# A decoder trunk in float32: attention scores one step further ahead of their transposes, with a larger scratch ring for the weights

## The chip, the core and the metric

One core of one Trainium2 chip runs the whole program. The metric is device time in microseconds (us) of one execution, here the median of three runs. TensorE is called PE, its weight loads PEld, VectorE DVE, ScalarE ACT, GpSimd POOL, and SyncE (which only issues DMAs) SP.

## What is computed

Two layers, each of three blocks with a layer norm behind each: a SwiGLU feed-forward, a token mixer, a second SwiGLU feed-forward. The stream has 512 tokens of 1024 channels in float32. The change lies in the mixer alone. Its attention part, cut to what matters:

```python
# B: 12 heads of 64 in three dilated groups; A: 8 heads in 2 groups, selected and windowed keys
scores = q @ k.T * scale                  # per query block of 128
e = exp(scores - max) * mask
p = e / sum(e)                            # the attention weights
o = p @ v
# A's two branches are scaled by sigmoid gates and added, with a third over compressed keys;
# the groups of B are merged by their softmax denominators
```

Beside it the mixer has the input projections, a gated spatial unit (SGU), sigmoid gates over 3 x 1024 columns, and the merge. Every float32 product is made from halves: a high part rounded to fp32r and a low part, the remainder, so that one product is three matmuls (`mm3`, lines 461 to 463).

## The kernel before, in words

**Two streams in one.** `mixer` (1441) weaves two Python generators while the program is written out: `dense` (1415: compressed keys, B's projections for heads j = 0..3, A's for two groups, SGU, gates, merge) and `attn` (1424: the attention steps). `weave` (1461) emits one piece of attention, then dense pieces worth 1.5 (B) or 1.6 (A) times its estimated matmul time. If attention isn't ready, a dense piece is emitted; if dense can't go on, attention goes alone, and when both wait, the flag `force` lets attention skip its safety margin (960). Each engine executes its instructions in the order in which they were written, so this order is what counts.

**An attention step** is one head and one query block i = 0..3 of 128 rows. `pipe` (962) runs 16 B steps (j, i), then 32 A steps (h, i). One turn n of `pipe` does, in this order:

- the transposes of an older step m (`turn`, 966), if no P·V is pending;
- the scores of step n: matmuls on PE, masking and row minimum on DVE into a float32 tile E (B line 1549, A line 1652), then exp on ACT (1566, 1667);
- `finish` (971): a pending P·V (`pv`), m's transposes if still open, and `low(m)`: DVE's subtraction that makes the low half of the transposed weights (1602, 1704). The transposes' high half is an ACT cast (1593, 1691). When m has i = 3, the head's P·V is pending for the next turn;
- the normalisation of E by POOL (`scale`; 1572 for B in the same turn, 1676 for A in the next one).

Which older step m is taken is set by `lag`: the step whose scores lie `lag` turns back. While the next step's projections aren't there and `force` is on, lines 990 to 993 finish all live steps one after the other, whatever `lag` says. This is called a drain below.

```python
m = live.popleft() if live and n - live[0]["turn"] >= live[0]["f"].lag else None
...
if self.force and (m or live or pv):
    yield from finish(m or (live.popleft() if live else None))
```

**Scratch.** `Fa` has 76 blocks of 128 columns, 44 of its own and 32 that hold the stream until it is spilled to DRAM. E tiles are taken in a ring from its start: blocks 0..`EB` in B, 0..`EA` in A (1525, 1640). Dense's temporaries (rope, SGU, gates, the P·V accumulator `ev`) use a ring over the rest, `f_lo` to 76 (329), where `f_lo` is `EB`, then `EA`. A B step takes 3, 6, 8 or 10 blocks for i = 0..3, an A step 2, 4, 6 or 8; they are freed when its transposes are written out (1595, 1693).

**Around it.** POOL also makes the low half of the streamed mixer weights (390), 1024 columns at a time, and adds in rope (918, 934, 1104, 1106).

Of the kernel before, what the change touches and what calls it, by code (L numbers as in the profile page):

```python
# [230 lines left out]

RB, R0, FB = 232, 152, 44
HB = RB - R0
EB, EA = 30, 24
XB = NT * KT
RAW, WB, LOOK = 3, 4, 8
MARGIN, RATIO_B, RATIO_A = 6.0, 1.5, 1.6
# [4 lines left out]
class Trunk:  # L242
# [719 lines left out]
    def pipe(self, steps):  # L962

        live, pv = deque(), None

        def turn(m):
            m["f"].transposes(m)
            m["turned"] = True
            yield m["f"].t_cost(m)

        def finish(m):
            nonlocal pv
            if pv:
                yield from pv["f"].pv(pv["step"])
                pv = None
            if m:
                if not m["turned"]:
                    yield from turn(m)
                m["f"].low(m)
                if m["step"][-1] == NT - 1:  # L980
                    pv = m

        for n, (f, step) in enumerate(steps + [(None, None)] * 4):
            if live and live[-1]["turn"] == n - 1 and live[-1]["f"].late:
                live[-1]["f"].scale(live[-1])
            m = live.popleft() if live and n - live[0]["turn"] >= live[0]["f"].lag else None
            if m and not pv:
                yield from turn(m)
            if f:
                while not f.ready(*step):  # L990
                    if self.force and (m or live or pv):
                        yield from finish(m or (live.popleft() if live else None))
                        m = None
                    else:
                        yield WAIT
                while (s := f.scores(*step)) is None:
                    yield WAIT
                s.update(f=f, step=step, turn=n, turned=False)
                live.append(s)
                self.ratio = f.ratio  # L1000
                yield f.s_cost(s)
                f.exps(s)
            yield from finish(m)
            if f and not f.late:
                f.scale(s)
        yield from finish(None)
# [499 lines left out]

class StepsB:

    lag, late, ratio = 2, 0, RATIO_B

    def __init__(self, t):
        self.t = t
# [112 lines left out]

class StepsA:

    lag, late, ratio = 3, 1, RATIO_A

    def __init__(self, t):  # L1630
        self.t = t
# [131 lines left out]
```

## Time and profile before

| | before |
|---|---|
| three runs | 2710.33, 2713.63, 2713.87 us |
| median | 2713.63 us |
| the profiled execution's own time | 2713.97 us |
| its span, first to last instruction | 2711.9 us |
| PE busy in the span | 96% |
| DVE, ACT, POOL busy | 65%, 45%, 45% |
| mean granted clock of PE | 0.989 of full speed |

The feed-forwards are dense matmul work and fill about 1.6 ms of the span. The two mixers lie at about 370 to 910 us and 1720 to 2280 us; the attention steps in them run from 428 to 800 us and from 1776 to 2150 us. A share of the span is an average over both kinds of stage, so the attention stretches are to be read by themselves.

### The profile page before, as it was taken

The page shows a single profiled execution, that of the slowest core. Times are in us where ns is not written, and L with a number is a line of the kernel's source. Part 1 is how long each engine was busy: PE and PEld are TensorE (multiplying, and loading weights), DVE is VectorE, ACT ScalarE, POOL GpSimd, SP SyncE. Part 2 cuts the span into 40 slices and gives each one's busy share as a digit, 9 for nine tenths or more (in the row PEclk, how much of TensorE's full clock was granted, in tenths as well). Part 3 has the DMA queues.
Part 4 walks back from the last instruction along what each step waited for, and adds up shares of the span by engine and source line. Part 5 has one row for each costly group of instructions (what it writes and reads, how often), then busy time and mean ns, then how long its engine had stood idle before and what let it go on. Part 6 is the DMA issues. An engine that isn't in the chain of part 4 may idle for free.

```text
span 2711.9 us, 42598 instructions
## 1 busy us (share of the span) xinstructions
PE 2611.7 (96%) x16302; PEld 2346.8 (87%) x16302; DVE 1776.2 (65%) x3155; ACT 1209.4 (45%) x2410; POOL 1223.9 (45%) x961
## 2 busy tenths in 40 slices
PE   8999999989999999999999999999899999999998
PEld 7999888877788888998889998888777888889987
DVE  6887565567552378885688875755674424698856
ACT  4555344345642235554345553334455422355542
POOL 4774025454645426770057720345446445277600
PEclk9999999999999999999999999999999999999999
DMA  3334322121212332333223342321112123323332
GB/s 132 102 110 144 100 98 96 37 71 39 71 42 85 108 132 86 109 102 126 77 86 110 102 134 91 110 77 60 47 40 74 45 91 115 118 94 102 109 117 78
DMA packets 71211, 248.68 MB, mean 92 GB/s; under 512 B 8016, under 2 KB 10096, under 8 KB 71008
## 3 DMA queue, kind: packets, MB, share of 16 engines
q1 hardware_dynamic: 68832, 238.25, 26.5%
q0 software_dynamic: 2176, 7.71, 0.9%
q8 instruction: 128, 2.10, 0.3%
q14 instruction: 75, 0.61, 0.1%
HBM read 239.64 MB, written 6.29 MB: 91 GB/s over the span
## 4 chain that ended last, share of the span: by engine, by line
PE 82%; DVE 11%; ACT 3%; issue 2%; POOL 2%; DMA 0%; DVEq 0%; ACTq 0%; SPq 0%; POOLq 0%
PE P L461 25%; PE P L462 25%; PE P L463 25%; DVE wl L390 2%; PE P L1722 1%; PE P L1615 1%; POOL wl L390 1%; DVE R L575 1%; DVE Fa L1549 1%; DVE Fa L631 1%; PE P L1686 1%; PE P L1651 1%; PE P L886 1%; ACT wh L387 1%; PE P L1588 1%
## 5 line engine op out<-in xcount | busy, mean ns | idle before, releaser
L461 PE MATMUL P<-R,wh 128*128 128x256 f32 (+1 forms) x2928 | 891.4, 304 | 8.0 <-ACT Fa L817 6.4
L463 PE MATMUL P<-R,wl 128*128 128x256 f32 (+1 forms) x2928 | 890.5, 304 | 6.9 <-DVE wl L390 6.4
L462 PE MATMUL P<-R,wh 128*128 128x256 f32 (+1 forms) x2928 | 888.6, 303 | 7.0 <-DVE R L541 6.9
L387 ACT CAST wh<-raw 128x1024 fp32r<-128x1024 f32 (+3 forms) x521 | 431.3, 833 | 508.4 <-PE P L463 248.1
L390 POOL TENSOR_TENSOR wl<-raw,wh 128x1024 fp32r<-128x1024 f32 (+4 forms) x159 | 357.2, 2254 | 660.8 <-ACT wh L387 660.2
L390 DVE TENSOR_TENSOR wl<-raw,wh 128x512 fp32r<-128x512 f32 (+2 forms) x363 | 422.2, 1166 | 312.5 <-ACT wh L387 312.2
L463 PEld LDWEIGHTS P<-R,wl 128*128 128x128 f32 x2928 | 560.9, 192 | 33.6 <-DVE wl L390 11.7
L461 PE MATMUL P<-wh,R 128*128 128x512 f32 (+3 forms) x1600 | 583.6, 365 | 6.5 <-DVE R L893 5.6
L461 PEld LDWEIGHTS P<-R,wh 128*128 128x128 f32 x2928 | 561.0, 192 | 32.8 <-ACT Fa L817 8.4
L462 PEld LDWEIGHTS P<-R,wh 128*128 128x128 f32 x2928 | 561.0, 192 | 30.2 <-DVE R L541 9.0
L463 PE MATMUL P<-wh,R 128*128 128x512 f32 (+3 forms) x1600 | 573.1, 358 | 4.4 <-DVE R L541 4.2
L462 PE MATMUL P<-wl,R 128*128 128x512 f32 (+3 forms) x1600 | 573.0, 358 | 4.1 <-POOL wl L390 2.1
L390 DVE TENSOR_TENSOR wl<-Fa,wh 128x512 fp32r<-128x512 f32 x304 | 353.1, 1163 | 87.0 <-ACT wh L387 87.0
L461 PEld LDWEIGHTS P<-wh,R 128*128 128x128 f32 x1600 | 305.0, 191 | 45.9 <-issue 6.6
L463 PEld LDWEIGHTS P<-wh,R 128*128 128x128 f32 x1600 | 304.2, 190 | 46.3 <-DVE R L541 5.3
L462 PEld LDWEIGHTS P<-wl,R 128*128 128x128 f32 x1600 | 304.9, 191 | 43.5 <-POOL wl L390 3.1
L408 POOL TENSOR_TENSOR Fa<-raw 128x512 f32<-128x512 f32 x152 | 227.0, 1493 | 194.5 <-DMA raw<-in_wts 96.5
L387 ACT CAST wh<-Fa 128x512 fp32r<-128x512 f32 x304 | 180.9, 617 | 4.4 <-POOL Fa L408 4.4
L834 ACT ACTIVATE Fa<-Fa 128x512 f32<-128x512 f32 x76 | 48.0, 632 | 242.3 <-DVE Fa L832 242.3
L408 POOL TENSOR_TENSOR Fa<-raw,Fa 128x512 f32<-128x512 f32 x76 | 131.9, 1735 | 3.7 <-DVE wl L390 3.7
L408 POOL TENSOR_TENSOR Fa<-Fa,raw 128x512 f32<-128x512 f32 x76 | 117.0, 1540 | 6.0
L1676 POOL TENSOR_SCALAR Fa<-Fa,ac,ga 128x128 f32<-128x128 f32 (+3 forms) x128 | 78.8, 627 | 84.4 <-DVE ac L1672 83.9
(222 smaller groups left out, 3144.4 us busy)
## 6 DMA issues: line engine op xcount, KB each, us to landing
raw<-in_wts SPq DMA_DIRECT2D x400, 512.0 KB, 3.3
raw<-in_wts SPq DMA_DIRECT2D x16, 480.0 KB, 3.2
x_sp<-Fa SPq DMA_DIRECT2D x8, 512.0 KB, 5.2
Fa<-x_sp SPq DMA_DIRECT2D x8, 512.0 KB, 5.3
Fa<-in_ln_g POOLq DMA_DIRECT2D x6, 512.0 KB, 4.4
Fa<-in_ln_b POOLq DMA_DIRECT2D x6, 512.0 KB, 5.6
raw<-in_wts SPq DMA_DIRECT2D x8, 320.0 KB, 3.0
Fa<-in_x SPq DMA_DIRECT2D x4, 512.0 KB, 7.2
```

The lines of the kernel that those rows point to most:

```text
L387: nc.scalar.copy(h, r)
L390: (nc.gpsimd if kind == "full" and (self.pool_lo or j == 1) else nc.vector).tensor_tensor(lo, r, hf, op=OP.subtract)
L408: self.nc.gpsimd.tensor_tensor(v, x, y, op=op)
L461: mm(out, lh, rh, start=start, stop=False, skip_group_check=more)
L462: mm(out, lh, rl, start=False, stop=False, skip_group_check=more)
L463: mm(out, ll, rh, start=False, stop=stop, skip_group_check=more)
L575: nc.vector.tensor_tensor(lo, t[n], hif, op=OP.subtract)
L631: self.nc.vector.scalar_tensor_tensor(xs[:, c], xs[:, c], r, b[:, c], op0=OP.mult, op1=OP.add)
L834: nc.scalar.activation(st["g"], st["g"], AF.Silu)
L886: self.nc.tensor.transpose(self.P[b][:s.shape[-1], k * 128:(k + 1) * 128], s, self.ident)
L1549: nc.vector.tensor_tensor_reduce(E[:, at:at + n], P, m, -SCALE, 3e38 if g == 0 else acc[:, g - 1:g], OP.add, OP.min, acc[:, g:g + 1])
L1676: t.nc.gpsimd.tensor_scalar(e, e, rd[:, br:br + 1], t.ga[:, s["i"], c:c + 1], op0=OP.mult, op1=OP.mult)
```

## The change

B's `lag` goes from 2 to 3 and A's from 3 to 4, so each step's transposes, casts, low halves and P·V are written one turn later against the scores. The E ring grows from 30 to 40 blocks in B and from 24 to 32 in A, and dense's ring, which starts where it ends, shrinks from 46 to 36 and from 52 to 44 blocks. `pipe` runs one empty turn more at its end. No instruction of the computation is added or taken away.

```diff
-EB, EA = 30, 24
+EB, EA = 40, 32
...
-        for n, (f, step) in enumerate(steps + [(None, None)] * 4):
+        for n, (f, step) in enumerate(steps + [(None, None)] * 5):
...
 class StepsB:
 
-    lag, late, ratio = 2, 0, RATIO_B
+    lag, late, ratio = 3, 0, RATIO_B
...
 class StepsA:
 
-    lag, late, ratio = 3, 1, RATIO_A
+    lag, late, ratio = 4, 1, RATIO_A
```

## Rows read from the trace of the kernel before

**Rows 1.** The page: busy us, share of the span, instructions; then the chain's shares.

```profile
PE 2611.7 (96%) x16302; PEld 2346.8 (87%) x16302; DVE 1776.2 (65%) x3155; ACT 1209.4 (45%) x2410; POOL 1223.9 (45%) x961
...
PE 82%; DVE 11%; ACT 3%; issue 2%; POOL 2%; DMA 0%; DVEq 0%; ACTq 0%; SPq 0%; POOLq 0%
```

**Rows 2.** PE's waits over the span: line, releaser: us in total, times, longest.

```profile
PE P L1615 <- DVE R L1602: 12.3, 4, 4.3
PE P L1588 <- POOL Fa L1572: 9.9, 8, 2.1
...
PE P L1722 <- DVE R L1704: 5.8, 10, 1.4
```

**Rows 3.** PE in time, B steps: start, us, instruction, [idle before, releaser], layer 1.

```profile
466.98 2.89 PE L1615 MATMUL P<-R,Rb 128*128 128x512 f32 x11 [1.92 <-DVE R L1602]
...
498.35 2.01 PE L1588 MATMUL P<-ident,Fa 128*128 128x128 f32 x10 [2.12 <-POOL Fa L1572]
...
518.98 0.67 PE L1588 MATMUL P<-ident,Fa 128*128 128x128 f32 x3 [1.99 <-DVE Rb L893]
...
533.96 1.31 PE L1588 MATMUL P<-ident,Fa 128*128 128x128 f32 x10 [1.09 <-POOL Fa L1572]
...
585.45 1.31 PE L1588 MATMUL P<-ident,Fa 128*128 128x128 f32 x10 [1.49 <-POOL Fa L1572]
...
598.65 6.17 PE L1615 MATMUL P<-R,Rb 128*128 128x512 f32 x23 [4.28 <-DVE R L1602]
```

**Rows 4.** Windows: start:end, us, busy PE, PEld, DVE, ACT, POOL, PE's clock, DMA.

```profile
460.00:472.00 12.00, 9.89 (x62) 8.32 (x60) 7.01 (x25) 4.94 (x11) 5.81 (x5) 0.86 0.25 82
496.00:502.00 6.00, 3.88 (x22) 3.66 (x20) 3.29 (x8) 1.97 (x5) 2.98 (x3) 0.73 0.39 139
532.00:538.00 6.00, 4.91 (x36) 4.60 (x36) 4.23 (x13) 2.97 (x9) 2.03 (x3) 1.00 0.01 3
```

**Rows 5.** POOL in time, around the second head's last B step.

```profile
491.80 2.28 POOL L390 TENSOR_TENSOR wl<-raw,wh 128x960 fp32r<-128x960 f32 x1
...
494.73 2.25 POOL L390 TENSOR_TENSOR wl<-raw,wh 128x960 fp32r<-128x960 f32 x1
496.95 1.34 POOL L1572 TENSOR_SCALAR Fa<-Fa,ac 128x1280 f32<-128x1280 f32 x1
```

**Rows 6.** PE in time: six transposes; one matmul of a projection.

```profile
439.21 0.90 PE L1588 MATMUL P<-ident,Fa 128*128 128x128 f32 x6
...
448.30 0.28 PE L461 MATMUL P<-wh,R 128*128 128x256 f32 x1
```

**Rows 7.** DVE in time, ahead of the fourth head's P·V.

```profile
592.90 2.14 DVE L1226 TENSOR_SCALAR ac<-ac 128x4 f32<-128x4 f32 x1
...
597.58 1.61 DVE L1602 TENSOR_TENSOR R<-P,R 128x256 fp32r<-128x256 f32 x3
```

**Rows 8.** POOL in time, the same stretch.

```profile
592.64 4.67 POOL L390 TENSOR_TENSOR wl<-raw,wh 128x1024 fp32r<-128x1024 f32 x2 [0.64 <-ACT wh L387]
```

**Rows 9.** PE in time, A steps: waits of transposes (1686) and of P·V (1722).

```profile
700.86 0.66 PE L1686 MATMUL P<-ident,Fa 128*128 128x128 f32 x4 [0.36 <-POOL Fa L1676]
...
701.85 0.66 PE L1686 MATMUL P<-ident,Fa 128*128 128x128 f32 x4 [0.33 <-POOL Fa L1676]
...
731.00 0.49 PE L1722 MATMUL P<-R 128*128 128x512 f32 x1 [0.73 <-ACT R L1691]
...
732.87 0.50 PE L1722 MATMUL P<-R 128*128 128x512 f32 x1 [1.38 <-DVE R L1704]
```

**Rows 10.** PE in time: the shortest and the longest scores of an A step.

```profile
583.40 0.56 PE L1651 MATMUL P<-R,Rb 128*128 128x128 f32 x4
...
631.20 1.17 PE L1651 MATMUL P<-R,Rb 128*128 128x512 f32 x4
```

**Rows 11.** DVE in time: one mask-and-minimum of an A step with 384 and with 512 columns.

```profile
731.18 0.55 DVE L1652 CUSTOM_DVE_ANT_0 Fa<-P,masks 128x384 f32<-128x384 f32 x1
...
733.74 0.69 DVE L1652 CUSTOM_DVE_ANT_0 Fa<-P,masks 128x512 f32<-128x512 f32 x1
```

## The prediction

> **What bounds the kernel now.** I read the page first: PE is busy for 96% of the span, and the chain that ended last runs over PE for 82% and over DVE for 11% [rows 1]. So time can be won in two ways: PE waits less, or its clock falls less often. The span has 2711.9 - 2611.7 = 100.2 us in which PE is idle. Then I read PE's waits, to see which of them the change can touch [rows 2]. Two belong to B: P·V waiting for the low halves from DVE (12.3 us), and transposes waiting for POOL's normalisation (9.9 us in 8 waits). A's P·V waits for the low halves from DVE for 5.8 us, in 10 waits. Third, I put PE in order of time over the attention steps of layer 1 [rows 3] and looked up the granted clock of the stretches around the longest waits [rows 4]. [...] After the wait of 1.09 us before 533.96 the clock stays at 1.00. [...]
>
> The transposes' wait is a matter of order on POOL. The normalisation of the second head's last step takes 1.34 us, but starts only at 496.95, behind two weight splits of 2.28 and 2.25 us [rows 5], while PE stands before the transposes of that same step.
>
> **The change, part by part.** No instruction is added or removed. What moves by one turn is, for every step, its transposes (PE), the casts behind them (ACT), the low halves (DVE), and for every head its P·V and `o_evac`. Scores, exp, reciprocal and normalisation stay where they are against each other on PE, ACT, DVE and POOL. SP's queue holds no DMA of an attention step; weight DMAs go out when splits are written, by the same clock of estimated costs.
>
> *B's transposes against POOL.* The waits of layer 1 come to 9.9 / 2 = 4.95 us; the three large ones are 2.12, 1.09 and 1.49 us, and each stands before a head's last, ten-transpose step [rows 3]. Two of them (heads 2 and 3) are in drains: the next head's projections aren't there, so the lag doesn't hold, and the last step's transposes follow its own scores as soon as the steps before it are emptied. With the lag of 3 one more step is still live, so one more group of six transposes (0.90 us busy) and the projection piece that the weave puts behind it, 12 matmuls of 0.28 us busy each, which overlap, come in between [rows 6]. That is between 0.9 and 0.9 + 12 x 0.28 = 4.3 us of PE work; I take it to cover 2.12 us, since the weave has a debt of 1.5 times each attention piece. The wait before 585.45 is no drain: there a full turn comes in. I take all 4.95 us as gone, and the clock's 1.6 us behind the first of them: 6.5 us a layer. Bounds: at the least, only the wait outside a drain goes (1.5 us), at the most 6.5 us.
>
> *A's transposes against POOL.* 0.36 + 0.33 = 0.7 us a layer [rows 9]; a further turn of at least one score piece of 0.56 us lies ahead of each [rows 10]. I take 0.7 us, bounds 0 and 0.7.
>
> *P·V against the low halves, B.* Where P·V waits for 1.92 and 4.28 us [rows 3], it is written straight behind the low halves, in stretches where dense can't go on because the blocks for the next head's values, or for A's keys, are not free. With the change the same thing comes one step later; P·V is still written straight behind `low`. I count no gain. What delays DVE before the second of them is seen in its own rows: an operation on 128 x 4 elements took 2.14 us, and the low halves began at 597.58 [rows 7], while POOL was in weight splits from 592.64 for 4.67 us [rows 8]. [...] The first of the two could also get longer, as attention goes alone for one step more: I bound that by a second wait like it, 1.92 + 1.7 = 3.6 us a layer, and take 0, since that step's own inputs are long there.
>
> *P·V against the low halves, A.* Before, a head's P·V stands behind the scores of the next head's last block; afterwards behind those of the first block of the head after that. PE's cover shrinks from 1.17 to 0.56 us [rows 10], by 0.6 us, and DVE has two minima of 512 columns ahead of the low halves where it had two of 384, 2 x (0.69 - 0.55) = 0.3 us [rows 11]. That is 0.9 us for a P·V with no dense piece beside it. Seven heads of a layer have such a successor; the waits of this kind (10 over both layers, [rows 2]) show that in a layer about three have nothing to hide it, among them the one with 0.73 + 1.38 us [rows 9]. I take 3 x 0.9 = 2.7 us a layer; bounds 0 and 7 x 0.9 = 6.3 us.
>
> *Scratch.* The larger E ring lets the scores of one more step be held: at most 3 + 6 + 8 + 10 = 27 of 40 blocks in B, 2 + 4 + 6 + 8 + 2 = 22 of 32 in A. Dense's ring shrinks. Its peak by the code is in `spatial`: six gates, the gate parameters, two u, y and `ev`, (6 + 1 + 2 + 1 + 1) x 4 = 44 blocks, and the ring has 76 - 32 = 44. It just fits if nothing lies across a multiple of four, so I take 0. [...]
>
> **Sum.** A layer: -6.5 - 0.7 + 2.7 = -4.5 us; two layers: -9.0 us. Against the profiled execution's own 2713.97 us this gives 2705.0 us; that execution is 0.3 us above the median of 2713.63 us, so 2704.6 us against the runs. I forecast 2704.6 us.
>
> **Rivals.**
>
> *The waits only move* (chance 0.24): PE reaches the next DVE result earlier and waits there. For it: DVE is the other engine on the chain [rows 1], and one wait before transposes, 1.99 us before 518.98, is for DVE and not for POOL [rows 3]. Against it: in these 6 us windows DVE is busy for 3.29 and 4.23 us [rows 4], so it has room. Half of the gain lost and the price of A kept: 2 x (-3.6 + 2.7) = -1.8, some 2712 us.
>
> *P·V of A becomes the bound* (0.16; slower): the place is the turn behind each head, from the point where the low halves end later than the scores of 0.56 us. All seven pay 0.9 us, 6.3 us a layer, and two waits grow long enough (the trace's 1.9 us are) for the lower clock, 2 x 1.7 us. With half of the gain: 2 x (-3.6 + 6.3 + 3.4) = +12 us, 2726 us; with the whole of it 2719 us. I name 2720 us.
>
> *Dense's ring is too small* (0.08): one block lies across, dense stops in `spatial` until attention ends, and the last steps of attention run alone. 48 steps take 428 to 800 us, 7.8 us each, so three of them some 23 us. The stretch 460 to 472, which did, lost 2.1 us idle and 1.7 us of clock in 12 us [rows 4]: some 23 / 12 x 3.8 = 7 us a layer. 2 x (7 - 4.5) = +5, 2719 us.
>
> That the change doesn't do what it says is part of the first rival: drains take no notice of the lag.
>
> **How the numbers follow.** The forecast has the remaining 0.52. Down, its bounds are 2 x (-6.5 - 0.7) = -14.4 us, and if the 1.99 us before 518.98 go too, with their clock, 2 x 3.6 us more: 2692 us. Up, the range takes in the first rival and the middle of the slower ones, 2721 us. A measurement can tell about 0.2%, 5.4 us, from no change. Faster by more than that: most of the forecast (0.48) and a little of the first rival (0.05), 0.53. Slower: 0.16 of the second, 0.04 of the third, 0.20. Between them 0.27.
>
> **What would show it.** Right: in PE's waits the row for B's transposes on POOL falls from 9.9 us to under 2; the clock around the second head's last transposes stays at 1.00; the rows for P·V on DVE's low halves in B stay near 12 us, those in A grow from 5.8 us to some 10. Wrong: the POOL row stays (the drains decide), the A row passes 20 us (second rival), or PE's idle time before the projections names scratch released late (third). New waits of 1.9 us or more at places that I don't name, each with some 1.7 us of low clock, would move the time either way without any of these steps.

## The result: 0.78% slower, and the profile after

The changed kernel takes 2733.93 us (median of four runs, 2731.93 to 2735.28) against 2713.65 us for the kernel before (four runs now, three ahead of the prediction): a ratio of 1.0078, 95% interval 1.0066 to 1.0091. The prediction was 2704.6 us with 2721 us as its upper end. It was wrong, in sign as well as in size. The execution profiled after took 2734.74 us, its span is 2732.7 us and the mean granted clock 0.984 (before 0.989).

The page after, first line of its first part; this answers to [rows 1]. PE has 12.3 us more of busy time for the same 16302 instructions, at the lower mean clock (by an estimate from it 2732.7 x (1 - 0.984) = some 44 us are lost to it, before some 30 us), and 8.5 us more of idle time (2732.7 - 2624.0 = 108.7 us, before 100.2 us).

```profile
PE 2624.0 (96%) x16302; PEld 2354.6 (86%) x16302; DVE 1772.1 (65%) x3155; ACT 1214.2 (44%) x2410; POOL 1225.7 (45%) x961
```

PE's waits after, over the whole span, those that concern the mixer; this answers to [rows 2]. Columns: line, releaser, us in total, times, longest.

```profile
PE P L463 <- DVE R L893: 11.5, 4, 3.2
PE P L1722 <- DVE R L1704: 10.4, 9, 3.6
...
PE P L1615 <- DVE R L1602: 6.2, 6, 1.4
...
PE P L1588 <- DVE ac L1652: 5.5, 4, 2.5
...
PE P L1588 <- DVE Rb L478: 4.6, 4, 1.7
...
PE P L1686 <- DVE Fa L1034: 4.2, 2, 2.1
...
PE P L1686 <- DVE R L478: 3.4, 4, 1.3
```

The wait of B's transposes on POOL (9.9 us in [rows 2]) is gone, as predicted. Not as predicted, B's P·V on the low halves, which was to stay near 12 us, falls from 12.3 to 6.2 us. New or longer are transposes of B (1588) and of A (1686) that wait for DVE instructions which have nothing to do with them: line 478 makes the low half of A's values (the last row stood at 0.9 us before), 1034 is the SGU's gelu, 1652 a row minimum. A transpose writes into a PSUM bank, and by the order in which the program hands out its eight banks (271, 315) these are the instructions that read the bank's previous content. So the releaser's line says whose bank it was, not whose data. The longest row (463 for 893) stood at 5.6 us on line 461 before: its wait of 3.2 us in layer 1 lies where 2.8 us lay, one of 2.5 us at 593 us is new.

Windows of layer 1, first of the kernel before, then after. Columns: start:end, length, busy PE, PEld, DVE, ACT, POOL, PE's clock, DMA share, GB/s. The first stretch holds three of B's heads, the second B's end and A's projections, the third the rest of A's steps beside the SGU.

```profile
400.00:560.00 160.00, 150.35 (x1096) 141.33 (x1095) 85.57 (x275) 65.32 (x155) 83.32 (x79) 0.97 0.22 71
560.00:640.00 80.00, 70.90 (x394) 60.02 (x393) 56.96 (x181) 40.07 (x115) 35.59 (x43) 0.96 0.11 35
640.00:820.00 180.00, 170.05 (x876) 140.51 (x875) 99.63 (x266) 94.95 (x217) 97.64 (x90) 0.98 0.18 60
```

```profile
400.00:560.00 160.00, 153.26 (x1114) 142.71 (x1114) 86.50 (x286) 65.63 (x158) 84.16 (x80) 0.98 0.23 75
560.00:640.00 80.00, 69.22 (x368) 57.16 (x367) 53.11 (x173) 40.36 (x116) 37.51 (x44) 0.94 0.08 27
640.00:824.00 184.00, 169.53 (x860) 140.68 (x859) 101.14 (x260) 93.61 (x211) 93.06 (x87) 0.96 0.18 59
```

PE's idle time goes from 9.7 to 6.7 us in the first stretch: the predicted gain is there, in part. It is given back in the second (9.1 to 10.8 us, clock 0.96 to 0.94) and more than that in the third (10.0 to 14.5 us, clock 0.98 to 0.96).

To say where the time went in each run I use one length, that of a mixer from its first copy on ACT (line 1056) to its first merge product on DVE (1399). Before it is 448.4 us in layer 1 and 448.5 us in layer 2; after it is 454.4 and 464.6 us. The sum, 22.1 us more, covers the whole difference of the spans (20.8 us). That the layers differ by 10 us is the second thing to explain.

### The profile page after: what moved, and what is told of

It is laid out like the page before. It is cut to its first block, busy times and chain, and to the rows that moved or that the text cites. A ratio compares the mean times of both kernels' runs of the same rounds, so it can differ in the third digit from the quotient of the medians.

```text
span 2732.7 us, 42538 instructions
## 1 busy us (share of the span) xinstructions
PE 2624.0 (96%) x16302; PEld 2354.6 (86%) x16302; DVE 1772.1 (65%) x3155; ACT 1214.2 (44%) x2410; POOL 1225.7 (45%) x961
## 5 line engine op out<-in xcount | busy, mean ns | idle before, releaser
L408 POOL TENSOR_TENSOR Fa<-raw 128x512 f32<-128x512 f32 x152 | 225.4, 1483 | 192.2 <-DMA raw<-in_wts 104.3
```

What stands on the lines that cost most here:

```text
L408: self.nc.gpsimd.tensor_tensor(v, x, y, op=op)
```

## The experiments

Ratios are to the kernel before, timed beside each run on the same chip (its medians there: 2710.9 to 2713.7 us). "Mixers" are the two lengths just defined, from the one execution of each run that was profiled; e18's is its fastest, 6.0 us below its median, and e1's its slowest, 3.3 us above.

| run | what differs from the kernel before | median us | ratio, 95% interval | mixers, us |
|---|---|---|---|---|
| after | both lags, rings 40/32 | 2733.93 | 1.0078 [1.0066, 1.0091] | 454.4, 464.6 |
| e1 | B's lag | 2715.11 | 1.0018 [1.0009, 1.0027] | 449.3, 448.7 |
| e2 | A's lag | 2727.55 | 1.0065 [1.0053, 1.0078] | 456.2, 456.2 |
| e3 | rings 40/32 | 2713.51 | 1.0009 [1.0000, 1.0018] | 448.1, 447.9 |
| e4 | both lags, rings 40/24 | 2727.48 | 1.0063 [1.0051, 1.0076] | 454.3, 456.3 |
| e5 | A's lag, mask split on POOL | 2719.02 | 1.0024 [1.0015, 1.0033] | 450.7, 451.0 |
| e6 | halves | 2706.17 | 0.9971 [0.9959, 0.9983] | 451.0, 445.0 |
| e7 | both lags, rings 40/24, halves | 2712.23 | 0.9997 [0.9989, 1.0006] | 449.7, 449.2 |
| e8 | A's ratio 1.5 | 2727.59 | 1.0056 [1.0044, 1.0068] | 457.7, 452.6 |
| e9 | mask split on POOL | 2718.32 | 1.0020 [1.0009, 1.0031] | 449.8, 452.3 |
| e10 | B's lag, subtraction on POOL | 2719.31 | 1.0024 [1.0014, 1.0035] | 450.7, 452.4 |
| e11 | subtraction on POOL | 2719.24 | 1.0021 [1.0012, 1.0029] | 450.4, 452.1 |
| e12 | B's lag, halves, both moves to POOL | 2718.18 | 1.0021 [1.0012, 1.0031] | 452.8, 452.0 |
| e13 | splits on DVE | 2728.30 | 1.0060 [1.0047, 1.0072] | 461.0, 459.7 |
| e14 | both lags, rings 40/24, splits on DVE | 2765.74 | 1.0199 [1.0185, 1.0213] | 480.8, 481.0 |
| e15 | B's lag, splits on DVE | 2747.01 | 1.0127 [1.0112, 1.0143] | 471.0, 471.9 |
| e16 | B's lag, halves | 2715.42 | 1.0009 [1.0000, 1.0017] | 450.4, 451.6 |
| e17 | B's lag for three heads of four | 2706.40 | 0.9981 [0.9973, 0.9990] | 445.3, 445.0 |
| e18 | A's lag, halves | 2708.68 | 0.9996 [0.9986, 1.0005] | 444.9, 446.6 |

### The change in its parts (e1 to e4)

```diff
e1 and e4:  EB, EA = 40, 24      e2:  EB, EA = 30, 24      e3:  EB, EA = 40, 32
e1:  StepsB.lag = 3              e2:  StepsA.lag = 4       e3:  no lag changed      e4:  both lags
```

> B's lag of 3 with its ring of 40 blocks; A's lag and ring stay at 3 and 24. If the lag pays in B, as the trace of the changed kernel has it (B's transposes no longer wait for POOL, some 4.5 us a layer less up to 550 us): about 9 us under the kernel before, 2705 us. If the smaller ring of the dense stream costs and the lag is neutral: within 3 us of 2713.7, since dense keeps its 52 blocks in A. If any shift only deals the waits anew: somewhere between 2703 and 2724.

> A's lag of 4 alone, with the old rings of 30 and 24 blocks; B as before. If A's lag is what costs (the waits of layer 1 from 618 us on grow from 11 to 16.5 us, with one more stretch of low clock, some 9 us a layer): 2728 to 2735 us. If the ring costs and the lag is neutral: 2711 to 2717. If waits are only dealt anew: 2703 to 2724.

> The rings of 40 and 32 blocks with the old lags of 2 and 3. By the order of allocation the spatial unit of layer 2 finds no four blocks in a row here, as in the changed kernel, and dense stops until attention ends. If that is what costs: 8 us more than before, 2722 us, all of it in layer 2 between 2110 and 2310 us. If it were the whole of the loss: 2730 or more. If the lag is the whole of it: 2711 to 2717.

> The changed kernel with A's ring back at 24 blocks, in which the lag of 4 still fits, so that dense has 52 blocks again. If the blocked spatial unit of layer 2 costs 8.5 us and the lags the rest: 2725 us, both layers some 7 us longer than before. If the ring is the whole of the loss: 2705 to 2714.

A's lag alone costs 7.8 and 7.7 us in the two mixers. B's lag alone is about neutral there (+0.9 and +0.2 us), and the rings alone cost nothing (-0.3 and -0.6 us). The three parts don't add up to the change: with both lags and the roomy A ring (e4) the layers cost +5.9 and +7.8 us, and the ring of 32 on top of that adds nothing in layer 1 but 8.3 us in layer 2 (464.6 against 456.3).

This last part is the third rival. The E ring and dense's ring start each layer where the layer before left them. Followed through the program's own allocations, in layer 2 the four blocks of the gate parameters come to lie off the multiple of four, at 54. When `spatial` asks for its last four, four are free (52, 53, 62 and 63) but not in a row, and it gets them only when attention ends. PE in time and the window there, in the changed kernel:

```profile
2139.30 4.53 PE L1722 MATMUL P<-R 128*128 128x512 f32 x15 [3.62 <-DVE R L1704]
...
2130.00:2155.00 25.00, 19.72 (x90) 16.08 (x91) 13.41 (x34) 10.87 (x26) 8.22 (x11) 0.80 0.02 6
```

and the same window with the A ring of 24 (e4):

```profile
2130.00:2155.00 25.00, 23.12 (x134) 19.27 (x131) 15.90 (x38) 15.14 (x34) 16.13 (x15) 1.00 0.08 27
```

Attention runs alone, P·V has nothing ahead of it and waits 3.62 us, and the clock of the stretch falls to 0.80. In e3 the same blocks lie the same way in layer 2, and dense stops at the same request. There attention's lone end comes at 2110 to 2130 us: PE idles 2.8 us in it (0.8 us before), but its longest wait is 1.49 us, the clock stays at 1.00, and the mixer is no longer than before. So the stop alone is cheap, and it is the lag of 4 that makes it dear. What the old lags have ahead of these P·V was not tried.

### What A's lag meets (e5, e9, e8)

Of the 4 us that e2 idles more between 640 and 830 us, P·V has almost nothing: its two rows there come to 2.9 + 1.4 us before and 3.0 + 1.5 us with the lag. The new waits are mostly those of transposes (2.1 and 1.1 us in e2). In the changed kernel, PE, DVE and POOL in time:

```profile
651.07 1.54 PE L1686 MATMUL P<-ident,Fa 128*128 128x128 f32 x6 [1.28 <-DVE R L478]
...
700.68 0.55 PE L1686 MATMUL P<-ident,Fa 128*128 128x128 f32 x3 [2.09 <-DVE Fa L1034]
...
645.00 2.40 DVE L1229 TENSOR_TENSOR Fa<-Fa,ac 128x128 f32<-128x128 f32 x1
...
696.72 2.58 DVE L481 CAST R<-Fa 128x512 fp32r<-128x512 f32 x1 [3.61 <-POOL Fa L1318]
...
699.94 0.68 DVE L1034 SCALAR_TENSOR_TENSOR Fa<-Fa,P 128x512 f32<-128x512 f32 x1
...
696.04 0.64 POOL L1318 TENSOR_SCALAR_AFFINE_SELECT Fa<-Fa 128x512 f32<-128x512 f32 x1
696.66 2.36 POOL L390 TENSOR_TENSOR wl<-raw,wh 128x1024 fp32r<-128x1024 f32 x1
```

The same cast in the kernel before, and POOL beside it:

```profile
696.68 0.43 DVE L481 CAST R<-Fa 128x512 fp32r<-128x512 f32 x1 [3.34 <-POOL Fa L1318]
697.14 0.69 DVE L482 TENSOR_TENSOR R<-Fa,R 128x512 fp32r<-128x512 f32 x1
...
696.01 0.64 POOL L1318 TENSOR_SCALAR_AFFINE_SELECT Fa<-Fa 128x512 f32<-128x512 f32 x1
697.25 2.80 POOL L390 TENSOR_TENSOR wl<-raw,wh 128x1024 fp32r<-128x1024 f32 x1 [0.60 <-ACT wh L387]
```

This is the mask of the SGU's spatial weights (POOL, 1318) and the cast behind it (DVE, 481). Before, POOL's next weight split had to wait 0.60 us for its high half from ACT; the cast took 0.43 us and was over when the split started. The subtraction behind it (482) started 0.11 us ahead of the split and kept its 0.69 us, and the split took 2.80 us. After, with the pieces of the weave dealt differently, the high half was there, the split started 0.06 us ahead of the cast, and the cast took 2.58 us: until 0.28 us after the split's end. Behind it in DVE's queue stood the gelu that frees the bank for which the transposes waited 2.09 us, and the window 700 to 712 has a clock of 0.72, where the window 694 to 706 of the kernel before has 1.00:

```profile
700.00:712.00 12.00, 10.61 (x40) 8.71 (x41) 6.11 (x20) 3.21 (x8) 3.24 (x5) 0.72 0.13 45
```

```profile
694.00:706.00 12.00, 10.79 (x61) 8.64 (x60) 6.77 (x22) 6.68 (x18) 10.38 (x10) 1.00 0.39 137
```

The test is to take this cast and its subtraction off DVE, under the new lag and under the old. The expectations call this reading, that a DVE operation is held by a split of POOL that it meets, the port theory. The name stands for the times above alone (2.58 us beside the split, 0.43 us ahead of it): no run shows what makes the one wait for the other.

```diff
-        self.hilo_sb(self.rv(wsR, 4), self.rvf(wsR, 4), self.rv(wsR + 4, 4), ws)
+        nc.gpsimd.tensor_scalar(self.rv(wsR, 4), ws, 1.0, 1.0, op0=OP.mult, op1=OP.mult)
+        nc.gpsimd.tensor_tensor(self.rv(wsR + 4, 4), ws, self.rvf(wsR, 4), op=OP.subtract)
```

> Edit: the run with A's lag of 4 alone (2727.55 us), with the split of the SGU's spatial weights (a cast and a subtraction of 128x512, once a layer) written on POOL and no longer on DVE. Port theory: that cast took 2.57 us on DVE because it met a weight split of POOL, PE's transposes stood for it 2.07 us, and the clock fell behind it; without the cast on DVE a layer loses 2.1 us of wait and 1.7 to 3.4 us of clock less, 7.6 to 11 us over both layers: 2716.5 to 2720 us. P·V theory (the lag's cost lies in P·V behind shorter scores): no change, 2727 us. Dealt-anew theory (any change of order costs this much): no change or a new wait elsewhere, 2725 to 2732 us.

> Edit: the kernel before (both lags and rings as they were), with the split of the SGU's spatial weights written on POOL as in the run that brought A's lag from 2727.55 to 2719.02 us. Port theory: in the kernel before this cast starts ahead of POOL's split and takes 0.43 us, so nothing is to be won: 2709 to 2715 us (before 2712), and the gain of 8.5 us belongs to the lag of 4 alone. Rival (the edit helps every order): 2702 to 2706 us.

With the lag of 4 it gives back 0.0041 of the 0.0065 (11 us; the two mixers get 5.5 and 5.2 us shorter). With the lag of 3 nothing was to be won, and it costs 5.4 us, 3 us more than the upper end of what was expected: POOL's normalisation now stands behind two more instructions and a split. POOL and PE in time in e9 (its line 1677 is 1676 of before, 1687 is 1686):

```profile
694.19 0.62 POOL L1321 TENSOR_SCALAR R<-Fa 128x512 fp32r<-128x512 f32 x1
694.89 1.28 POOL L1322 TENSOR_TENSOR R<-Fa,R 128x512 fp32r<-128x512 f32 x1
696.13 2.36 POOL L390 TENSOR_TENSOR wl<-raw,wh 128x1024 fp32r<-128x1024 f32 x1
698.48 1.68 POOL L1677 TENSOR_SCALAR Fa<-Fa,ac,ga 128x512 f32<-128x512 f32 x2
...
699.47 1.40 PE L1687 MATMUL P<-ident,Fa 128*128 128x128 f32 x8 [2.34 <-POOL Fa L1677]
```

In e5 this wait is absent: there the lag of 4 does what it is for. So without this cast on DVE the two lags stand at 1.0024 and 1.0020, where they were 0.0065 apart; 0.0020 of the difference is what the edit costs the old lag.

e8 changes no lag, only the deal: 1.5 dense pieces for each of A's in place of 1.6.

```diff
-MARGIN, RATIO_B, RATIO_A = 6.0, 1.5, 1.6
+MARGIN, RATIO_B, RATIO_A = 6.0, 1.5, 1.5
```

> Edit: the kernel before, with the ratio of dense work to A's steps at 1.5 where it was 1.6; lags and rings as before. Dealt-anew theory (any other pairing of attention pieces with dense pieces costs, since the old one was fitted to the waits): slower by 5 to 16 us, 2716 to 2727 us. Port and P·V theories (the lag itself matters): within 4 us of the kernel before, 2707 to 2715 us.

It costs 15 us, as the dealt-anew theory said, and the same collision is in its trace: PE, DVE and POOL in time.

```profile
704.43 1.09 PE L1686 MATMUL P<-ident,Fa 128*128 128x128 f32 x4 [4.92 <-DVE Fa L1034]
...
700.40 2.56 DVE L481 CAST R<-Fa 128x512 fp32r<-128x512 f32 x1 [2.67 <-POOL Fa L1318]
...
700.34 2.33 POOL L390 TENSOR_TENSOR wl<-raw,wh 128x1024 fp32r<-128x1024 f32 x1
```

The two theories meet here, but not any new order costs, and who is first is no toss-up. In every run with the cast on DVE and splits on POOL the cast starts 0.03 to 0.04 us after the mask's end. With A's lag of 4 (after, e2, e4, e7, e18) and in e8 the next split's high half is there, the split follows the mask at once, and the cast is held (1.50 to 2.72 us), in both layers. With the old lag of A and the ratio of 1.6 (before, e1, e3, e6, e10, e11, e16, e17) the split comes 0.12 to 0.66 us later and the cast takes 0.43 us, in both layers, although B's order is another in half of them.

### Shorter splits (e6, e7, e18, e16)

```diff
+SPLIT = 2
...
-        (nc.gpsimd if kind == "full" and (self.pool_lo or j == 1) else nc.vector).tensor_tensor(lo, r, hf, op=OP.subtract)
+        if kind == "full" and (self.pool_lo or j == 1):
+            for c in range(0, w, w // SPLIT):
+                cs = slice(c, c + w // SPLIT)
+                nc.gpsimd.tensor_tensor(lo[:, cs], r[:, cs], hf[:, cs], op=OP.subtract)
+        else:
+            nc.vector.tensor_tensor(lo, r, hf, op=OP.subtract)
```

> Edit: the kernel before, with each weight split of POOL written as two instructions of half the columns. Port theory: a DVE instruction on two SBUF operands, or a cast, that meets a split is held for at most some 1.2 us where it was 2.1 to 2.6 us; in the kernel before the wait of 4.28 us before 598.65 and that of 2.8 us before 648 get 1 us shorter each and some clock comes back: 2 to 4 us a layer, 2704 to 2708 us (before 2711). Rival: POOL's splits cost more in two parts and the normalisations behind them come later, or the waits don't depend on it: 2711 to 2716 us.

> Edit: both lags raised, E ring of A at 24 (2727.48 us), with each weight split of POOL as two instructions of half the columns. Port theory: the cast of 2.6 us and the small operations before 650 are held for half as long, waits of 2 to 3 us shorten by about 1 us and some stay too short for the clock to fall: 5 to 8 us a layer back, 2712 to 2718 us; the distance to the kernel before with half splits shrinks from 16.5 to under 8 us. P·V theory: 2725 to 2728 us, distance as before. Dealt-anew theory: distance 10 to 20 us.

> Edit: the run with A's lag of 4 alone (2727.55 us), with POOL's weight splits in halves (the kernel before with halves: 2706.17 us). Port theory: the cast of the spatial weights is held for at most some 1.3 us, the distance to the old lag falls from 15 us to under 6: 2706 to 2712 us. If the lag itself costs (P·V, banks): 2716 to 2724 us.

> Edit: B's lag of 3 alone, its ring 40, with POOL's weight splits in halves (the kernel before with halves: 2706.17 us). Port theory: shorter holds give less back, so B's gain shows: 2699 to 2705 us. If the gain is taken back by the order itself: 2706 to 2712 us.

e6 is faster than the kernel before by 0.29%, e7's distance to it is 0.0026 (7 us, was 0.0063), e18's 0.0025 (was 0.0065): about what the port theory said, a little above its 6 us for e18. But only in part by the way that I had named.

In e6 the two named waits do get 1 us shorter (4.28 to 3.1 us, 2.83 to 1.9 us), but B's transposes wait longer for POOL up to 560 us (6.1 us, before 3.5), and the two mixers together are as long as before (896.0 and 896.9 us). What the profiled execution gains lies behind the mixers' first merge products: the stretch up to the second mixer takes 896.5 us (before 899.6), the one behind it 542.4 us (543.9). PE's wait for the low half of the transposed stream in the feed-forwards (462 for 541) falls from 6.9 us, longest 1.9, to 3.6 us, longest 0.7. e7, e12, e16 and e18 have the first of these stretches at 896.3 to 897.1 us as well.

In e7 and e18 the cast was still held, 2.72 us in e7 (first line, with POOL's two halves beside it) and 1.50 us in e18 (second; 2.72 us in its layer 2):

```profile
692.11 2.72 DVE L487 CAST R<-Fa 128x512 fp32r<-128x512 f32 x1 [4.09 <-POOL Fa L1324]
...
692.02 2.52 POOL L394 TENSOR_TENSOR wl<-raw,wh 128x512 fp32r<-128x512 f32 x2
```

```profile
687.98 1.50 DVE L487 CAST R<-Fa 128x512 fp32r<-128x512 f32 x1 [3.86 <-POOL Fa L1324]
```

and the transposes behind it waited 2.8 and 2.5 us. What got shorter is the other place, the small operations around 645 us: lines 1226, 1228 and 1229 took 2.02, 2.09 and 2.40 us in the changed kernel and take 0.91, 0.99 and 1.34 us in e7, and PE's wait of 3.2 us behind them (463 for 893) is no longer among the waits of e7 and e18 from 640 to 830 us. e16 missed: with halves B's lag stands 0.0038 (10 us) above e6, further than without them (0.0018).

### Where B's gain went (e10, e11, e12, e17)

In e1 a subtraction of 128x128 was held for 3.08 us and PE waited 3.34 us for what stood behind it. PE, DVE and POOL in time:

```profile
658.50 0.82 PE L1686 MATMUL P<-ident,Fa 128*128 128x128 f32 x4 [3.34 <-DVE R L1704]
...
654.67 3.08 DVE L1219 TENSOR_TENSOR Fa<-Fa,ac 128x128 f32<-128x128 f32 x1
...
654.59 2.33 POOL L390 TENSOR_TENSOR wl<-raw,wh 128x1024 fp32r<-128x1024 f32 x1
```

The hold itself isn't the lag's: in the kernel before the same subtraction takes as long, and PE waits 0.18 us behind it, since it comes later.

```profile
652.76 3.10 DVE L1219 TENSOR_TENSOR Fa<-Fa,ac 128x128 f32<-128x128 f32 x1
...
656.60 0.63 PE L1686 MATMUL P<-ident,Fa 128*128 128x128 f32 x4 [0.18 <-DVE R L1704]
```

So here the first rival is seen: PE reaches the same DVE result earlier and waits there. I moved the subtraction to POOL, under the new lag of B and under the old, and then with everything at once (e12, with B's lag of 3: this, halves and the mask split).

```diff
-        nc.vector.tensor_tensor(v(E), v(E), bc(m), op=OP.subtract)
+        nc.gpsimd.tensor_tensor(v(E), v(E), bc(m), op=OP.subtract)
```

> Edit: the run with B's lag of 3 alone (2715.11 us), with the subtraction of the row maximum in the compressed scores (128x128, 16 of them) on POOL and no longer on DVE. Port theory: in that run one of these subtractions was held for 3.08 us behind a split and PE stood 3.34 us for what DVE had queued behind it, another for 1.60 us with a wait of 1.71 us of PE, in each layer; without them on DVE 3 to 5 us a layer come back: 2705 to 2709 us. Rival (B's gain is given back by the order of its drains, whoever does the subtraction): 2713 to 2717 us.

> Edit: the kernel before, with the subtraction of the row maximum in the compressed scores on POOL. Port theory: two of these subtractions took 1.7 us in the mean there too, but PE had no wait behind them; 2709 to 2714 us. Rival (the edit helps every order): 2702 to 2708 us, as much as with B's lag.

> [...] Port theory: B's own gain (2.6 us of idle time up to 560 us and 1.7 us of clock, in each layer) is no longer given back: 2694 to 2702 us, below the kernel before with halves (2706). Rival (each edit moves the collisions on): 2704 to 2712 us.

All three missed: they are 5 to 6.4 us slower than the kernel before. In e10, DVE, POOL and PE in time:

```profile
651.00 0.29 DVE L1217 TENSOR_REDUCE ac<-Fa 128x4 f32<-128x128 f32 x1
...
651.22 2.38 POOL L390 TENSOR_TENSOR wl<-raw,wh 128x1024 fp32r<-128x1024 f32 x1
...
654.96 0.39 POOL L1219 TENSOR_TENSOR Fa<-Fa,ac 128x128 f32<-128x128 f32 x1
...
657.75 1.54 PE L886 MATMUL P<-ident,Fa 128*128 128x128 f32 x6 [2.51 <-DVE Rb L893]
```

The subtraction, ready at 651.29, starts at 654.96, behind a split and two additions of rope; the chain that it belongs to comes later by as much as DVE was held before, and e10 and e11 have a new wait of 2.5 and 2.6 us before other transposes (886). In the chain ahead of it, at 641 us, lines 1228 and 1229 are held for 2.12 and 2.40 us (before, 1226 and 1228 for 2.02 and 2.05), and PE's wait behind them is 3.9 us in both runs where it was 2.8 us. Moving a held instruction to the engine that holds it was no way out here.

e17 asks for the place instead. With the lag of 3, B's last steps are still live when A's projections and first scores come. In e1, e16 and the changed kernel transposes of B wait there for banks, first at 577 to 582 us for 2.4 us and then at 590 to 595 us for 1.5 to 1.7 us. So B's lag is put back to 2 for its last head.

```diff
+            lag = lambda m: m["f"].lag - (m["f"].late == 0 and m["step"][0] == 3)
+            while live and n - live[0]["turn"] > lag(live[0]):
+                yield from finish(live.popleft())
-            m = live.popleft() if live and n - live[0]["turn"] >= live[0]["f"].lag else None
+            m = live.popleft() if live and n - live[0]["turn"] >= lag(live[0]) else None
```

> Edit: the run with B's lag of 3 alone (2715.11 us), with the lag of B back at 2 for its last head, so that the way from B to A is as in the kernel before. Order theory (B's gain is given back by its last steps, which meet A's projections): the gain up to 560 us stays (2 to 4 us a layer of idle time and clock) and nothing is given back: 2703 to 2709 us. Rival (any new order finds its own waits on DVE): 2711 to 2718 us.

```profile
400.00:560.00 160.00, 153.21 (x1119) 143.38 (x1118) 85.41 (x283) 66.21 (x157) 83.66 (x79) 0.98 0.23 75
560.00:640.00 80.00, 71.42 (x389) 60.49 (x388) 56.24 (x177) 41.67 (x118) 38.46 (x45) 0.94 0.08 28
640.00:820.00 180.00, 170.04 (x872) 140.64 (x871) 100.22 (x266) 92.89 (x212) 95.32 (x88) 0.98 0.18 60
```

The gain of the first stretch stays (6.8 us idle, before 9.7), the second has the old waits again (1.56, 1.49 and 4.20 us; 8.6 us idle, before 9.1), and the third is as before (10.0 us; in e1 12.9): the subtraction is held for 3.10 us here too, and PE waits 0.19 us behind it. Both mixers are 3 us shorter, and the kernel is 0.19% faster than before. So the gain of B's first three heads was given back by the longer lag of its last head, by the waits on the way from B to A and by what they shift behind them, and not by B's steps as such. What each of these waits costs by itself wasn't taken apart.

### No split on POOL inside the mixers (e13 to e15)

`POOL_LO` is how many of every eight weight splits written between the mixer's pieces go to POOL.

```diff
-SPACE, POOL_LO, AHEAD = 2.0, 8, 1
+SPACE, POOL_LO, AHEAD = 2.0, 0, 1
```

> Edit: the kernel before, with all weight splits inside the mixer on DVE and none on POOL. It is the base for the next two. Port theory: no DVE instruction is held behind a split and POOL's normalisations come at once, but DVE has some 1.27 us more for each split (the mean of such a split on DVE): waits of PE on DVE grow or shrink, 2700 to 2730 us; the waits of transposes on POOL (3.5 us up to 560 us) go. Rival: nothing of this, the waits on POOL stay.

> Edit: both lags raised, A's ring 24, with all weight splits inside the mixer on DVE. Port theory: within 6 us of the run before it (with the splits on POOL the distance is 15 to 16.5 us). Dealt-anew theory (any change of order costs): 10 to 20 us more than the run before it. P·V theory: as much.

> Edit: B's lag of 3 alone, its ring 40, with all weight splits inside the mixer on DVE. Port theory: without splits on POOL there is no wait on POOL for the lag to remove and no collision that takes it back: within 4 us of the base with splits on DVE, either side. If the order of B's drains takes the gain back: 4 to 10 us above the base.

This went against the port theory as I had put it. Without splits on POOL the lags cost not less but more: 18.7 us for B's, and 18.7 us more for A's. DVE is then fuller (104.3 us busy of the 160 from 400 to 560 us, 85.6 before), and P·V of A waits for the low halves already in e13. Its row from 640 to 840 us in e13 and in e14:

```profile
PE P L1722 <- DVE R L1704: 9.1, 5, 3.7
```

```profile
PE P L1722 <- DVE R L1704: 11.5, 7, 3.3
```

So the wait that the second rival named is long in that kernel with the old lags already, B's lag leaves it at 9.2 us (e15), and A's lag adds 2.3 us a layer, a quarter of its 18.7 us; where the rest goes wasn't taken apart. In the kernel of the change the row hardly moves. Two of B's new waits are unchanged by the missing splits (2.5 us on line 1652 and 2.5 us on 893, between 560 and 640 us in e15), so these come with the order and not with POOL's splits. The waits on POOL did not go in e13 either (3.0 us in three waits up to 560 us, 3.5 before): splits were only a part of why the normalisation is late.

## Why the prediction was wrong

The forecast was -4.5 us a layer; measured are +6.0 and +16.1 us. The sum failed at the terms that stand for moved work: each took the wait that goes and left out what the moved instructions meet.

**B's transposes against POOL (-6.5 us a layer): the waits went, the gain didn't stay.** The row of 9.9 us is gone, and PE idles 2.9 us less up to 560 us. The clock's 1.6 us in the prediction's term is an estimate from [rows 4], 6.00 x (1 - 0.73), as is the 1.7 us in its other sums, 12.00 x (1 - 0.86); in the same stretch from 496 us PE is busy for all of the 6.00 us after, at a clock of 1.00. But B's lag alone makes the mixers 0.9 and 0.2 us longer. The step that failed is "The wait before 585.45 is no drain: there a full turn comes in": I looked at what the turn covers and not at what the moved transposes meet. They meet the banks of A's scores and projections (2.43 us at 577, 1.65 us at 590 us), and behind that PE meets DVE results too early (in e1 3.34 us at 658 us). e17, which leaves that head alone, keeps 3 us a layer.

**P·V of B (0, "P·V is still written straight behind `low`"): also mis-sized, the other way.** The wait of 4.28 us before the fourth head's P·V is 1.17 us after, in layer 2 4.24 and 1.17 us. In the changed kernel, PE and DVE in time (before: [rows 3] and [rows 7]):

```profile
597.05 5.69 PE L1615 MATMUL P<-R,Rb 128*128 128x512 f32 x21 [1.17 <-DVE R L1602]
...
591.13 0.17 DVE L1226 TENSOR_SCALAR ac<-ac 128x4 f32<-128x4 f32 x1
```

The operations that were held for 2.14 us and, on line 1228, 2.05 us now meet no split. So the wait does depend on the order, against "I count no gain": with the last head's lag back at 2 (e17) it is 4.20 us again. The new waits beside it take the 3 us back.

**A's transposes against POOL (-0.7, bounds 0 and 0.7): this is the step that decided the sign.** "A further turn of at least one score piece lies ahead of each" is true, and those waits are gone. But a loss was left out of the bounds, without a row that excluded one: the term was a cost, and it had the wrong sign. Moved behind other dense pieces, the transposes ask for a bank that DVE still reads, and DVE is late where it met POOL (2.58 us for the cast, 2.40 us for line 1229): 2.1 us of wait at 700 us, 1.1 to 1.3 us at 651 us, and behind the first a clock of 0.72 in the 12 us from 700 us. Measured for the lag as a whole: +7.8 us a layer. With the one cast taken off DVE 5.5 and 5.2 us of that go (e5), and the two lags are 1 us apart (e5, e9).

**P·V of A (+2.7, bounds 0 and 6.3): mis-sized.** Between 640 and 830 us P·V waits 4.3 us before and 4.5 us with the lag (e2). DVE is busy there for 101.6 of the 190 us before, and the shorter cover cost 0.2 us. The row in the list of waits grew as forecast (5.8 to 10.4 us), but 3.6 us of that is the one P·V of layer 2 in the stretch without dense work: the right number for another reason, by luck.

**Scratch (0): right in layer 1, 8.3 us in layer 2.** "It just fits if nothing lies across a multiple of four" named the condition, and I took it as met without asking where a ring stands that is not set back between the layers. The third rival priced it at 7 us a layer; it came in one layer, and only together with the lags.

The parts, from the mixers: A's lag +15.5 us (e2), B's lag beside it -1.8 (e4 against e2), the ring of 32 with both lags +8.4 (after against e4): together the 22.1 us.

The last sentence of the prediction's working, that new waits of 1.9 us or more at places not named would move the time without any of its steps, is what happened: at 577 (2.43), 593 (2.53), 700 (2.09) and, in layer 2, 2139 us (3.62).

**Left open.** After e5's edit some 2.4 us a layer of A's lag remain against the kernel before; the wait at 651 us behind line 1229 is one part, the rest wasn't taken apart. Why halves of the splits help the old order and A's lag but not B's (e16) isn't settled.

## What to carry to other kernels

A longer distance between producer and consumer removes the wait that one sees (here 9.9 us), and moves everything behind it past other work: ask which buffer each moved instruction needs next (here a PSUM bank), who must free it, and how late that engine can be, and give the step a loss as well as a gain. Where two engines start behind the same event, ask which of them will have its other input ready: the cast at 697 us was quick (0.43 us) in every order tried in which POOL's next split still waited for its input, and held (1.50 to 2.72 us) in every one in which it didn't. An edit that changes no lag can cost as much as the one under study (e8, 15 us), so try it under a second order before crediting or blaming it. What paid here was to keep a gain and leave the place that gave it back untouched (e17), and to shorten the long holder (e6): 0.19% and 0.29% faster than the kernel before. And look where a gain lies: most of e6's is not in the mixers.

## What the runs showed of the hardware

In these traces an operation of DVE on two SBUF operands (482, 1219, 1228, 1229), a scalar operation (1226) or a float32 cast (481) from SBUF to SBUF did not run side by side with a weight split on POOL. Where they met, the one that started first kept its time and the other one lasted until about its end or longer: before, a subtraction (482) that led by 0.11 us kept its 0.69 us, and the split beside it took 2.80 us; after, a split that led by 0.06 us kept its 2.36 us, and the cast beside it, 0.43 us before, took 2.58 us. The subtraction of line 1219 lasted past the split's end: before, 3.10 us from 652.76 us, beside a split of 2.36 us from 652.66 and the addition of rope behind it (1104, 0.72 us from 654.99). A subtraction on DVE that reads PSUM kept its time (line 893 takes 0.28 us for 128x128 beside a split of POOL, in the kernel before at 639 us), and so did a row sum (1225, after, 0.29 us at 640.28 us beside a split from 640.22; 1226 behind it took 2.02 us).

What I had not expected is that a holder in two parts did not always let the other in between: in e7 the cast lasted 2.72 us although each half of a split takes some 1.3 us (two take 2.52 us); in layer 1 of e18 it lasted 1.50 us. And the hold didn't go by the size of the held instruction: [rows 7] show 2.14 us for 128x4 elements, which take 0.17 us where no split is met, and line 1229 above 2.40 us for 128x128. Nor were the splits the only holders: after, at 574.59 us, the operation of line 1226 took 1.24 us beside a normalisation of POOL (1572) that ran 1.33 us from 574.47. Beside one of A's (1676), at 591.13 us, it kept its 0.17 us; why isn't settled.

The clock's price is seen in pairs of windows: with the transposes' wait of 2.09 us the 12 us from 700 have a mean granted clock of 0.72, without it the 12 us around the same instructions have 1.00. After, in windows of 1 us, the clock is 0.50 from 702 to 708 us and 1.00 from 709; a matmul of 128x512 takes 0.63 us in the first stretch and 0.39 to 0.40 us in the second. By an estimate from the 0.72 the lower clock cost 12 x 0.28 = 3.4 us in these 12 us, more than the wait itself.
